# Seven more mixed pairs in the second half of two down projections, with row groups added into the residual stream by DMAs

## The chip, the cores and the metric

The program runs on one core of a Trainium2 chip. The metric is the device time of one execution in microseconds. The kernel before takes 2253.8 us (median of three runs, 2253.06 to 2253.91).

## What is computed

A decoder trunk over 256 tokens of width 2048 with two layers: an mLSTM layer and a differential-attention layer, each followed by a gated ConvFFN, with a residual stream `h` throughout and a final RMSNorm. The change touches only the ConvFFN's down projection (`@ w_down`, 5632 x 2048 in float32) and what is done with its result:

```python
def conv_ffn(xn, w_up, conv_w, conv_b, w_down):
    u = xn @ w_up
    ...                       # causal convolution of width 3 over the tokens
    gate, val = jnp.split(c, 2, axis=-1)
    return (jax.nn.silu(gate) * val) @ w_down

for layer in range(DEPTH):
    h = h + mixer_or_attention(h)
    h = h + conv_ffn(rms_norm(h, f_norm[layer]), w_up[layer], conv_w[layer], conv_b[layer], w_down[layer])
return rms_norm(h, final_norm)
```

## The kernel before

**Products in three passes.** Each float32 operand is split into a high part, rounded to the matmul's format, and the rest, so that a product is three matmuls: high by high, low by high, high by low. The activations are split once. The weights come in by `nc.sync` (queue SP) in blocks of 1 MB (`raw`, four buffers) and are split as they are needed: ACT copies the high part into a tile `w2` (five buffers), DVE subtracts it to get the low part (L376, L377 in `granule`).

**The down projection.** `conv_ffn` works in two halves of 22 k-tiles each (`part` 0 and 1). In each half the up projection makes `hidden[0..21]`, tiles of 128 channels by 256 tokens, and then `gemm_sevenths` makes the down product in groups `g` of 512 output columns, four groups a half. In the last layer's second half the fourth group is done otherwise (`finish`). A group's plain k-tiles go two at a time: twelve matmuls of 512 columns (L503) into two PSUM banks `a` and `b`, one for each half of the tokens.

**Seven products for eight.** A pair of k-tiles can be mixed instead: the pair, the two halves of the tokens and the two halves of the 512 columns make a 2 x 2 by 2 x 2 block product, which is done with seven block products where eight are usual. That is 21 matmuls of 256 columns (L493) in place of twelve of 512. Four sums of the hidden tiles are made ahead of it (`mix`), and four differences of the weights (`sevenths`: L449 to L451 on DVE into a buffer `diff` of the same four `raw` buffers). Seven weight blocks are then split instead of four: ACT L458 and DVE L459, three of them from `raw` and four from `diff`. `MIXED` names the k-tiles at which a mixed block of four k-tiles (two pairs) begins: 4, 12 and 20, the last with one pair only, so 10 of 22 k-tiles are mixed. Part of the mixed products goes into two more banks, `c` and `d` (`small_ps`, four such banks, which the transposes below use as well).

**Emptying a group.** `residual(norm)` returns the function that adds a finished group to `stream`, the residual in SBUF (128 tokens by 2 by 2048). `mixed_in` brings `c` and `d` in with one ACT copy (L572) and six DVE instructions (L573 to L579), and two more DVE adds (L587) bring in `a` and `b`. Then `norm.add(g)` begins the next layer's norm: two ACT squares of the new stream (L224), and in the next granule eight transposes on PE (L231), which ACT and DVE scale and split into `x_at` (L306, L307). In the last layer `evac_last` empties the groups; it makes the squares (L1074) and, two granules on, multiplies the stream by the final gain (L1075), with no transposes.

**The order.** `later(n, fn)` puts work off by `n` granules, counted by `tick()`. The Tile scheduler takes the program's order as priority and sets a fixed order for each engine; an engine runs its own queue in that order and waits on semaphores. Single matmuls, differences and adds of neighbouring blocks so come to stand between each other.

Of the kernel before, what the change touches and what calls it, by code (L numbers as in the profile page):

```python
# [37 lines left out]
NG = D // G  # L38
RAW = 4
OUT_AT = (8, 10)  # L40
MIXED = (4, 12, 20)
HL = 5
WARM, WARM_X = 28, 24
X_AT = (0, 2, 3, 5, 6, 8, 9)
# [24 lines left out]
def trunk(  # L69
# [394 lines left out]
    def gemm_sevenths(xs, mixed, w, col0, groups, evac, at):  # L464


        kn, raws = len(xs), {}
        for g in groups:
            a, b = (acc_ps.tile([P, 2 * T], F32, tag="acc", name="acc") for _ in range(2))
            c = d = None  # L470
            k0 = 0
            while k0 < kn:
                if k0 in at:
                    if c is None:
                        c, d = small_ps("mix"), small_ps("mix")
                    parts = sevenths(w, col0 + g * G, k0, min(2, (kn - k0) // 2))
                    for p, (b1, b2, b3, t1, t3, t2, t4) in enumerate(parts):
                        k = k0 + 2 * p
                        first, end = k == at[0], k0 == at[-1] and p == len(parts) - 1
                        (x0h, x0l, _), (x1h, x1l, _) = xs[k], xs[k + 1]  # L480
                        s1, s2, s3, s4 = mixed[k]
                        lo, hi = slice(0, P), slice(P, T)
                        c0, c1 = slice(0, T), slice(T, 2 * T)
                        ops = (((x0h[:, lo], x0l[:, lo]), b1, c[:, c0], first),
                               ((x1h[:, lo], x1l[:, lo]), b3, a[:, c1], False),
                               (s4, b2, a[:, c0], False),
                               (s1, t1, d[:, c0], first),
                               (s3, t3, d[:, c1], False),
                               (s2, t2, c[:, c1], False),
                               ((x1h[:, hi], x1l[:, hi]), t4, b[:, c1], False))  # L490
                        for (sh, sl), (th, tl), to, start in ops:
                            for o, (u, v) in enumerate(((sh, th), (sl, th), (sh, tl))):
                                pe.matmul(to, u, v, start=start and o == 0, stop=end and o == 2 and to is not a and to is not b, skip_group_check=True)  # L493
                        if p < len(parts) - 1:
                            tick()
                    k0 += 4
                else:
                    for i, (wh, wl) in enumerate(granule(w, col0 + g * G, G, k0, kn, raws, g)):
                        xh, xl, _ = xs[k0 + i]
                        for t, ps in enumerate((a, b)):  # L500
                            s = slice(t * P, (t + 1) * P)
                            for o, (u, v) in enumerate(((xh, wh), (xl, wh), (xh, wl))):
                                pe.matmul(ps, u[:, s], v, start=(k0 + i == 0 and o == 0), stop=(k0 + i == kn - 1 and o == 2), skip_group_check=True)  # L503
                    k0 += 2
                tick()
            evac(g, (a, b), (c, d))
# [71 lines left out]
        dve.tensor_tensor(both, both, u[1].rearrange("p (o n) -> p o n", o=1).broadcast_to([P, 2, T]), op=ALU.add)  # L578
        dve.tensor_tensor(stream[:, :, c0], d[:, :T].rearrange("p (o n) -> p o n", o=1).broadcast_to([P, 2, T]), stream[:, :, c0], op=ALU.add)  # L579

    def residual(norm):
        def evac(g, ps, mix=None):
            if mix is not None:
                mixed_in(g, mix)
            for t in range(2):
# [249 lines left out]
    def conv_ffn(layer, norm, evac_down, finish=None):  # L835
# [4 lines left out]
        for part in range(2):  # L840
# [20 lines left out]
            def evac_val(j, ps):  # L861
                pair = []
                for n in range(2):
# [5 lines left out]
                if 4 * (j // 2) in MIXED:  # L869
                    mixed[2 * j] = mix(pair)  # L870

            for j in range(half // 2):
# [1 line left out]
                gemm(norm.sets[0], w_up[layer], D_FF + part * half * P, [j], evac_val)  # L874
            rows = w_down[layer, part * half * P:(part + 1) * half * P]
            if part == 0:
                gemm_sevenths(hidden, mixed, rows, 0, range(NG), residual(None), MIXED)
            elif finish is None:
                gemm_sevenths(hidden, mixed, rows, 0, range(NG), evac_down, MIXED)
            else:  # L880
                gemm_sevenths(hidden, mixed, rows, 0, range(NG - 1), evac_down, MIXED)
                finish(hidden, rows)


# [156 lines left out]
    gemm_sevenths(outs, outs_mixed, m_w_out[0], 0, [NG - 1], residual(norm_f0), OUT_AT[:1])  # L1041

    norm_at = Norm([(gains, G_B), (gains, G_KV)], "at")
    conv_ffn(0, norm_f0, residual(norm_at))
    outs, outs_mixed = attention(norm_at)
    norm_f1 = Norm([(gains, G_F1)], "f1")
    gemm_tokens(outs, w_o[0], 0, range(2), residual(norm_f1), lead=2)
# [9 lines left out]
        return gain_rows[c0 // G][2][:, c0 % G:c0 % G + width]  # L1057

    def evac_last(g, ps, mix=None):
        if mix is not None:  # L1060
            mixed_in(g, mix)
# [6 lines left out]
        c0, width = g * G, G  # L1068
        if g == NG - 1:
            width = T  # L1070
        for t in range(2):
            rows = stream[:, t, c0:c0 + width]
            dve.tensor_tensor(rows, ps[t], rows, op=ALU.add)
            act.activation(tmp("sq").bitcast(BF16)[:, :width], rows, AF.Square, accum_out=norm_out.parts[:, t, g:g + 1])  # L1074
            later(2, lambda rows=rows: dve.tensor_tensor(rows, rows, gain_cols(c0, width), op=ALU.mult))  # L1075
        if g == NG - 1:
            later(1, sums_but_last)

    def sums_but_last():
        for t in range(2):  # L1080
# [60 lines left out]
```

## Time and profile before

| | |
|---|---|
| median of three runs | 2253.8 us |
| the profiled execution | 2253.21 us, span 2251.4 us, clock 0.999 |
| PE, DVE, ACT, POOL busy | 99%, 79%, 57%, 6% of the span |
| layer 0, second half: up projection | 761.45 to 1007.64 us |
| its down projection, groups 0 to 3 | 1007.64 to 1127.2 us |
| layer 1, second half: up projection | 1878.71 to 2124.20 us |
| its down projection, groups 0 to 2 | 2124.20 to 2212.41 us |

Times in the trace count from the first instruction. Busy PE counts matmuls, whose ends are modelled, since they are pipelined: how far apart they start says more than how long each is shown. A wait is put down to the engine, the line or the DMA whose semaphore came last.

### The profile page before, as it was taken

To read this page: it belongs to the slowest core of one execution; us is meant where nothing else is said; L and a number is where in the kernel's file an instruction comes from. 1 tells how busy PE (TensorE), PEld (TensorE's weight loads), DVE (VectorE), ACT (ScalarE), POOL (GpSimd) and SP (SyncE) were. 2 spreads that over 40 slices of the span, in tenths; PEclk is the share of its full clock that TensorE was granted. 3 is DMA by queue.
4 is the path that set the end of the run, shared out by engine and by line. 5 is a ranking of instruction groups with operands and counts; after the bars stand their busy time and mean duration, and the time that the engine had idled before them with its cause. 6 is when DMAs were issued, how large, how long until landed. Compare 5 with 4: busy or idle time off the path is not lost.

```text
span 2251.4 us, 33430 instructions
## 1 busy us (share of the span) xinstructions
PE 2239.6 (99%) x12843; PEld 1954.1 (87%) x12843; DVE 1789.7 (79%) x2964; ACT 1292.0 (57%) x1994; POOL 125.0 (6%) x305
## 2 busy tenths in 40 slices
PE   9999999999999999999999999999999999999998
PEld 9888888888888888888888888888888888888888
DVE  5756778887888877879998885677877988778896
ACT  5456655655555555656654556566555555556554
POOL 0014200000000000000022103200000000000000
PEclk9999999999999999999999999999999999999999
DMA  7554546555555755545566555465555457555464
GB/s 265 188 169 157 166 171 205 192 191 187 187 170 179 242 187 187 187 150 203 189 208 194 163 167 169 150 206 187 187 187 187 156 191 239 191 189 191 146 215 150
DMA packets 325348, 419.04 MB, mean 186 GB/s; under 512 B 9070, under 2 KB 238788, under 8 KB 325188
## 3 DMA queue, kind: packets, MB, share of 16 engines
q1 hardware_dynamic: 325156, 416.89, 56.4%
q8 instruction: 101, 1.65, 0.3%
q14 instruction: 59, 0.48, 0.1%
q10 hardware_dynamic: 32, 0.01, 0.0%
HBM read 414.77 MB, written 2.10 MB: 185 GB/s over the span
## 4 chain that ended last, share of the span: by engine, by line
PE 97%; DVE 1%; POOL 1%; issue 1%; ACT 0%; DMA 0%; DVEq 0%; SPq 0%; POOLq 0%
PE acc L411 54%; PE acc L503 16%; PE acc L437 12%; PE mix L493 6%; PE acc L493 4%; PE acc L634 2%; PE acc L521 1%; PE val_ps L335 1%; PE turn_ps L231 1%; PE as_ps L955 0%; DVE w L377 0%; POOL rs_u L279 0%; POOL rs_u L280 0%; DMA pos_i<-in_positions_dram 0%; POOL rs_u L281 0%
## 5 line engine op out<-in xcount | busy, mean ns | idle before, releaser
L377 DVE TENSOR_TENSOR w<-raw,w 128x1024 fp32r<-128x1024 f32 x679 | 825.9, 1220 | 280.1 <-ACT w L376 277.5
L376 ACT ACTIVATE w<-raw 128x1024 fp32r<-128x1024 f32 x679 | 713.9, 1058 | 491.7 <-PE acc L411 324.8
L411 PE MATMUL acc<-x_f,w 128*128 128x512 f32 (+1 forms) x5632 | 988.1, 337 | 0.0
L411 PEld LDWEIGHTS acc<-x_f,w 128*128 128x128 f32 x5632 | 861.7, 188 | 123.2
L503 PE MATMUL acc<-w,hid 128*128 128x512 f32 x1080 | 268.2, 394 | 0.0
L503 PEld LDWEIGHTS acc<-w,hid 128*128 128x128 f32 x1080 | 195.4, 188 | 39.0
L411 PE MATMUL acc<-x_at,w 128*128 128x512 f32 (+1 forms) x1024 | 182.1, 338 | 0.0
L411 PEld LDWEIGHTS acc<-x_at,w 128*128 128x128 f32 x1024 | 156.8, 188 | 22.2 <-issue 0.3
L458 ACT ACTIVATE w<-diff 128x1024 fp32r<-128x1024 f32 x89 | 94.1, 1057 | 111.1 <-DVE diff L451 81.7
L417 ACT ACTIVATE low<-acc 128x256 f32<-128x256 f32 x216 | 79.3, 386 | 135.4 <-PE acc L411 132.6
L459 DVE TENSOR_TENSOR w<-diff,w 128x1024 fp32r<-128x1024 f32 x89 | 108.7, 1221 | 40.9 <-ACT w L458 40.3
L437 PE MATMUL acc<-w,x_a 128*128 128x512 f32 x576 | 138.0, 396 | 0.0
L437 PEld LDWEIGHTS acc<-w,x_a 128*128 128x128 f32 x576 | 106.8, 188 | 24.2
L493 PE MATMUL mix<-w,mix 128*128 128x256 f32 x801 | 119.3, 281 | 0.0
L418 DVE TENSOR_TENSOR acc<-acc,low 128x256 f32<-128x256 f32 x216 | 84.5, 430 | 37.7 <-ACT low L417 37.3
L493 PEld LDWEIGHTS mix<-w,mix 128*128 128x128 f32 x801 | 107.0, 188 | 2.4 <-DVE w L459 0.2
L848 ACT ACTIVATE c<-u,conv 128x256 f32<-128x256 f32 x176 | 98.2, 593 | 5.5 <-DVE u L846 5.2
L939 POOL TENSOR_TENSOR sw<-sw,sin_t 32x256 f32<-32x256 f32 x32 | 42.0, 1328 | 1033.8 <-DVE sw L938 1022.5
L458 ACT ACTIVATE w<-raw 128x768 fp32r<-128x768 f32 x89 | 74.7, 840 | 37.9 <-PE acc L503 27.4
L437 PE MATMUL acc<-w,x_at 128*128 128x512 f32 x384 | 91.8, 396 | 0.0
L459 DVE TENSOR_TENSOR w<-raw,w 128x768 fp32r<-128x768 f32 x89 | 84.6, 951 | 2.8 <-ACT w L458 2.7
L493 PE MATMUL acc<-w,hid 128*128 128x256 f32 x450 | 86.3, 281 | 0.0
(302 smaller groups left out, 2320.4 us busy)
## 6 DMA issues: line engine op xcount, KB each, us to landing
raw<-in_w_up_dram SPq DMA_DIRECT2D x176, 1024.0 KB
raw<-in_w_down_dram SPq DMA_DIRECT2D x79, 1024.0 KB
raw<-in_m_w_in_dram SPq DMA_DIRECT2D x46, 1024.0 KB
raw<-in_w_kv_dram SPq DMA_DIRECT2D x32, 1024.0 KB
raw<-in_m_w_out_dram SPq DMA_DIRECT2D x16, 1024.0 KB
raw<-in_w_q_dram SPq DMA_DIRECT2D x16, 1024.0 KB
raw<-in_w_o_dram SPq DMA_DIRECT2D x16, 1024.0 KB
raw<-in_w_down_dram SPq DMA_DIRECT2D x15, 512.0 KB
```

Source lines behind the costliest of these rows:

```text
L376: act.activation(w2[:, :hc, 0], part, AF.Copy)
L377: dve.tensor_tensor(w2[:, :hc, 1], part, w2[:, :hc, 0].bitcast(F32), op=ALU.subtract)
L411: pe.matmul(to, a, b, start=(k == 0 and o == 0), stop=(k == kn - 1 and o == len(ops) - 1))
L417: act.activation(low, p[:, T:], AF.Copy)
L418: dve.tensor_tensor(p[:, :T], p[:, :T], low, op=ALU.add)
L437: pe.matmul(ps[t], a[:, s], b, start=(k == 0 and o == 0), stop=(k == kn - 1 and o == 2))
L458: act.activation(w2[:, :m, 0], src, AF.Copy)
L459: dve.tensor_tensor(w2[:, :m, 1], src, w2[:, :m, 0].bitcast(F32), op=ALU.subtract)
L493: pe.matmul(to, u, v, start=start and o == 0, stop=end and o == 2 and to is not a and to is not b, skip_group_check=True)
L503: pe.matmul(ps, u[:, s], v, start=(k0 + i == 0 and o == 0), stop=(k0 + i == kn - 1 and o == 2), skip_group_check=True)
L634: pe.matmul(ps[j], a, b, start=(k == 0 and o == 0 and j % 2 == 0), stop=(k == KD - 1 and o == 2), skip_group_check=True)
L848: act.activation(c, u, AF.Identity, bias=cw[:, 3, f:f + 1], scale=cw[:, 2, f:f + 1])
```

## The change

In the second halves the mixed blocks begin at k-tiles 2, 10 and 18, each with two pairs: 12 of 22 k-tiles instead of 10. The first halves stay as they are. A weight load covers the plain k-tiles between two mixed blocks, so a group has two plain ones in its first load (512 KB), then mixed blocks and plain blocks of four k-tiles in turn (1 MB each).

The first three groups of layer 0's second half and the first two of layer 1's are emptied by a new function, `landed`. ACT copies `a` and `b` into SBUF tiles, one ACT copy and four DVE adds make two more tiles from `c` and `d`, and four DMAs from POOL's queue add the four tiles into the stream. The norm's work on that group is put off by eight granules.

```diff
-MIXED = (4, 12, 20)
+MIXED = ((4, 12, 20), (2, 10, 18))
...
-                    for i, (wh, wl) in enumerate(granule(w, col0 + g * G, G, k0, kn, raws, g)):
+                    since = max([0] + [k + 4 for k in at if k < k0])
+                    until = min([kn] + [k for k in at if k > k0])
+                    for i, (wh, wl) in enumerate(granule(w[since * P:until * P], col0 + g * G, G, k0 - since, until - since, raws, g)):
...
+    def landed(g, ps, mix, then):
+        (a, b), (c, d) = ps, mix
+        u = tmp("mx")
+        a2, b2, x, y = (block(F32, f"land_{n}") for n in "abxy")
+        act.activation(x[1], c[:, :T], AF.Copy)
+        dve.tensor_tensor(u, c[:, T:], x[1], op=ALU.add)
+        act.activation(a2[2], a, AF.Copy)
+        dve.tensor_tensor(y[1], d[:, T:], u, op=ALU.add)
+        act.activation(b2[2], b, AF.Copy)
+        dve.tensor_tensor(x[0], d[:, :T], u, op=ALU.add)
+        dve.tensor_tensor(y[0], d[:, :T], y[1], op=ALU.add)
+        for t, rows in ((0, a2), (1, b2), (0, x), (1, y)):
+            pool.dma_start(stream[:, t, g * G:(g + 1) * G], rows[2], accum_op=ALU.add)
+        later(8, then)
...
-    def residual(norm):
+    def residual(norm, by_dma=0):
         def evac(g, ps, mix=None):
+            if g < by_dma:
+                landed(g, ps, mix, lambda: norm.add(g))
+                return
...
-    conv_ffn(0, norm_f0, residual(norm_at))
+    conv_ffn(0, norm_f0, residual(norm_at, 3))
...
     def evac_last(g, ps, mix=None):
...
+        if g < 2:
+            landed(g, ps, mix, lambda: summed(g, G))
+            return
```

Up to the second half of layer 0 every engine's order stays as it was. Three places show how the order changes.

DVE at the boundary between groups 0 and 1 of layer 0. `w_10062` and `w_10065` before, `w_10044` and `w_10047` after, are the first splits of group 1's first mixed block, from `raw` and from `diff`. Before:

```order
L459 TENSOR_TENSOR w_10062<-raw,w_10062 128x3x256
L451 TENSOR_TENSOR diff<-raw,diff 128x2x256
L573 TENSOR_TENSOR mixed<-mix,mixed 128x256
L575 TENSOR_TENSOR stream<-mix,stream 128x256
L574 TENSOR_TENSOR mixed<-mix,mixed 128x256
L576 TENSOR_TENSOR stream<-stream,mixed 128x256
L578 TENSOR_TENSOR stream<-stream,mixed 128x512
L459 TENSOR_TENSOR w_10065<-diff,w_10065 128x4x256
```

The same place after; L589 to L594 are `landed`:

```order
L459 TENSOR_TENSOR w_10044<-raw,w_10044 128x3x256
L450 TENSOR_TENSOR diff<-raw,diff 128x2x256
L589 TENSOR_TENSOR mx<-mix,land_x 128x256
L451 TENSOR_TENSOR diff<-raw,diff 128x2x256
L591 TENSOR_TENSOR land_y<-mix,mx 128x256
L593 TENSOR_TENSOR land_x<-mix,mx 128x256
L594 TENSOR_TENSOR land_y<-mix,land_y 128x256
L459 TENSOR_TENSOR w_10047<-diff,w_10047 128x4x256
```

The four adds of `landed` stand where five of the emptying's adds stood, and the adds of `a`, `b` and the rest, which followed later, are gone.

PE some 8 us into group 1 of layer 0, where the transposes of group 0's new stream (L231) stand. `w_10118` before and `w_10100` after are the split plain k-tiles behind the first mixed block. Before:

```order
L493 MATMUL acc<-w_10068,mix 128x256 x3
L503 MATMUL acc<-w_10118,hid_8427 128x512 x2
L493 MATMUL acc<-w_10071,hid_8218 128x256
L503 MATMUL acc<-w_10118,hid_8427 128x512 x2
L231 MATMUL turn_ps<-ident,stream 128x128 x2
L493 MATMUL mix<-w_10062,hid_7989 128x256 x3
L493 MATMUL mix<-w_10065,mix 128x256 x9
```

After (L505 is the line L503 of before):

```order
L505 MATMUL acc<-w_10100,hid_8217 128x512 x2
L493 MATMUL mix<-w_10053,mix 128x256 x5
L493 MATMUL acc<-w_10053,hid_8008 128x256
L505 MATMUL acc<-w_10100,hid_8217 128x512 x2
L231 MATMUL turn_ps<-ident,stream 128x128 x2
L493 MATMUL mix<-w_10136,hid_8637 128x256 x2
L231 MATMUL turn_ps<-ident,stream 128x128 x6
L505 MATMUL acc<-w_10100,hid_8217 128x512 x2
```

The transposes stand at about the same distance from the boundary as before, ahead of the matmuls with the low part of `w_10100`, and what they read now comes from the adding DMAs.

POOL, which has nothing in this stage before, now has the following rows (with the semaphores that each waits for; `DMASW0` and `DMASW1` are those of the first two DMAs; the last row belongs to group 1):

```order
L596 DMA stream<-land_a 128x512 [waits DVE_49,PE_49,Activation_49]
L596 DMA stream<-land_b 128x512 [waits DVE_49,PE_49,Activation_49]
L596 DMA stream<-land_x 128x512 [waits DMASW0_49,DVE_49]
L596 DMA stream<-land_y 128x512 [waits DMASW1_49,DVE_49]
L596 DMA stream<-land_a 128x512 [waits PE_49,Activation_49]
```

The third DMA waits for the landing of the first, the fourth for that of the second, since they add into the same rows.

More of the change, by code (lines that the diff above doesn't have):

```diff
@@ L868, in evac_val @@
                     pair.append(c)
-                if 4 * (j // 2) in MIXED:
+                if any(k <= 2 * j < k + 4 for k in MIXED[part]):
                     mixed[2 * j] = mix(pair)
@@ L876, in conv_ffn @@
             if part == 0:
-                gemm_sevenths(hidden, mixed, rows, 0, range(NG), residual(None), MIXED)
+                gemm_sevenths(hidden, mixed, rows, 0, range(NG), residual(None), MIXED[part])
             elif finish is None:
-                gemm_sevenths(hidden, mixed, rows, 0, range(NG), evac_down, MIXED)
+                gemm_sevenths(hidden, mixed, rows, 0, range(NG), evac_down, MIXED[part])
             else:
-                gemm_sevenths(hidden, mixed, rows, 0, range(NG - 1), evac_down, MIXED)
+                gemm_sevenths(hidden, mixed, rows, 0, range(NG - 1), evac_down, MIXED[part])
                 finish(hidden, rows)
@@ L1059, in evac_last @@
     def evac_last(g, ps, mix=None):
-        if mix is not None:
-            mixed_in(g, mix)
         if g == 0:
```

16 lines of the change are left out of this document (10 added, 6 removed).

## The prediction

> **What bounds the kernel now.** I read the page's busy shares and the shares of the chain that ended last, then the chain in order of time around the second half of layer 0's ConvFFN, then busy time by stage, the costs of the instructions that the change adds and removes, and last the traffic of the DMA engines and of POOL.
>
> The page (busy us, share of the span, count; below it the shares of the chain):
>
> ```profile
> span 2251.4 us, 33430 instructions
> PE 2239.6 (99%) x12843; PEld 1954.1 (87%) x12843; DVE 1789.7 (79%) x2964; ACT 1292.0 (57%) x1994; POOL 125.0 (6%) x305
> PE 97%; DVE 1%; POOL 1%; issue 1%; ACT 0%; DMA 0%; DVEq 0%; SPq 0%; POOLq 0%
> ```
>
> The end is set by TensorE. Time is saved only by taking matmul time away, and lost wherever PE is made to wait. The chain in order of time (start, length, what) shows what a matmul costs in the stage that is changed:
>
> ```profile
> 1007.64 5.59 PE acc L503 x24
> 1013.23 0.35 PE mix L493 x3
> ...
> 1018.19 0.94 PE acc L503 x4
> ...
> 1036.86 5.59 PE acc L503 x24
> ...
> 1045.52 0.22 PE turn_ps L231 x2
> ...
> 1067.00 5.58 PE acc L503 x24
> ```
>
> 24 plain matmuls take 5.59 us, so 0.2329 us each. The 42 matmuls of one mixed block of four k-tiles stand between 1013.23 and 1018.19: 4.96 us, 0.1181 each. The pieces join without a gap. A group is 72 plain and 105 mixed matmuls, 16.77 + 12.40 = 29.17 us; measured 29.22 from 1007.64 to 1036.86. The next group takes 30.14, since eight transposes (0.11 us each) stand in it.
>
> By stage (length; busy time and count of PE, PEld, DVE, ACT, POOL; clock; DMA share; GB/s), the up projection of layer 0's second half and its groups 0 to 2, then groups 0 and 1 of layer 1:
>
> ```profile
> 761.45:1007.64 246.19, 246.19 (x1408) 215.06 (x1407) 196.14 (x329) 144.92 (x222) 0.00 (x0) 1.00 0.59 193
> 1007.64:1036.86 29.22, 29.22 (x179) 25.95 (x178) 27.36 (x41) 17.36 (x23) 0.00 (x0) 1.00 0.53 178
> 1036.86:1067.00 30.14, 30.14 (x187) 26.85 (x186) 28.40 (x38) 19.60 (x28) 0.00 (x0) 1.00 0.53 178
> 1067.00:1097.12 30.12, 30.12 (x186) 26.84 (x186) 28.18 (x37) 19.41 (x28) 0.00 (x0) 1.00 0.58 192
> 2124.20:2153.31 29.11, 29.11 (x179) 25.91 (x178) 27.38 (x41) 17.37 (x23) 0.00 (x0) 1.00 0.53 176
> 2153.31:2182.50 29.19, 29.19 (x176) 25.82 (x175) 26.60 (x34) 17.56 (x23) 0.00 (x0) 1.00 0.63 211
> ```
>
> PE is full, and in the groups DVE is at 91 to 94%: a second engine stands close behind the first. POOL is idle here.
>
> **The change part by part.** *The matmuls.* In seven groups (four of layer 0, three of layer 1) one more pair of k-tiles is mixed: 12 plain matmuls go (2.795 us), 21 mixed ones come (2.480). That is 0.315 us a group, 2.2 us in all, straight from the path.
>
> *VectorE's work for it.* Groups of instructions (busy us, mean ns of one; the last row is from the instructions in order of time):
>
> ```profile
> L377 DVE TENSOR_TENSOR w<-raw,w 128x1024 fp32r<-128x1024 f32 x678 | 825.2, 1221 | 280.1 <-ACT w L376 277.5
> L459 DVE TENSOR_TENSOR w<-diff,w 128x1024 fp32r<-128x1024 f32 x89 | 108.7, 1221 | 40.9 <-ACT w L458 40.3
> L459 DVE TENSOR_TENSOR w<-raw,w 128x768 fp32r<-128x768 f32 x89 | 84.6, 951 | 2.8 <-ACT w L458 2.7
> L449 DVE TENSOR_TENSOR diff<-raw 128x1024 f32<-128x1024 f32 x37 | 45.1, 1219 | 4.2 <-DMA raw<-in_w_down_dram 3.3 <-DMA raw<-in_w_o_dram 0.8
> L451 DVE TENSOR_TENSOR diff<-raw,diff 128x512 f32<-128x512 f32 x37 | 25.3, 684 | 0.2
> L587 DVE TENSOR_TENSOR stream<-acc,stream 128x512 f32<-128x512 f32 x40 | 25.7, 682 | 0.1
> L573 DVE TENSOR_TENSOR mixed<-mix,mixed 128x256 f32<-128x256 f32 x20 | 8.3, 417 | 0.9 <-ACT mixed L572 0.8
> L572 ACT ACTIVATE mixed<-mix 128x256 f32<-128x256 f32 x20 | 7.6, 382 | 17.2 <-PE mix L493 17.2
> L224 ACT ACTIVATE sq<-stream 128x512 bf16<-128x512 f32 x32 | 19.7, 618 | 3.9 <-DVE stream L587 3.8
> 1015.43 2.35 DVE L377 TENSOR_TENSOR w<-raw,w 128x1024 fp32r<-128x1024 f32 x2
> ```
>
> The last row (two splits in 2.35 us) says that neighbours overlap by 0.09 us, so each counts as its mean less 0.09. A pair that becomes mixed drops one L377 (1.13) and adds two L459 (0.86 + 1.13) and a full set of differences in place of a half one (about +1.05): +1.9 us a group. Emptying a group costs now four DVE adds of 256 columns and four of 512 (L578, L579 and L587 twice, taken as 0.59 each): 1.31 + 2.36 = 3.7 us. An emptied-by-DMA group costs four of 256: 1.3. So where the adding DMAs come in, DVE gets 2.4 back for 1.9: 28.40 becomes about 27.9 in 29.8 us, still 94%. Group 0 has no emptying inside its window: 27.36 + 1.9 = 29.3 in 28.85. The cover there is the lead: the first mixed split of that group runs long before PE uses it at 1013.23:
>
> ```profile
> 1003.16 0.95 DVE L459 TENSOR_TENSOR w<-raw,w 128x768 fp32r<-128x768 f32 x1
> PEld mix L493 <- DVE w L459: 0.2, 1, 0.2
> ```
>
> A lead of 9 us pays an excess of 0.4, so group 0 costs nothing. The second row (layer 1's second half, the one wait of PE on a split) says that the lead does run out within a group: without the lead this term is on the path. ACT gets two copies of 512 columns for a group (2 x 0.62) and has 10 us idle in it: hidden. One more `mix` in each second half (about 2 us of DVE) lies in the up projection, where DVE is at 80%.
>
> *Just after a group boundary* DVE stands still until the last mixed matmul is done, since its landing adds now stand ahead of the first split by differences. From that matmul: ACT's `land_x` to 0.43, DVE's four adds and L451 to 2.4, ACT's difference split (behind `land_a` and `land_b`) to 2.7, then DVE: two L459 of differences, one of raw, one L449, and the split for k-tile 6 at 2.7 + 1.13 + 0.86 + 1.13 + 1.13 + 1.13 = 8.1. PE, by the new order, needs that split after 8 + 4 plain and 42 mixed matmuls: 7.75 us in layer 1, and 0.2 to 0.9 later in layer 0, where transposes stand ahead of it. Bounds: nothing (if the split comes 0.4 sooner than this count) to 1 us a group (if the adds wait for `land_x` as long again). I take 0.4 in two groups of layer 1: +0.8 us.
>
> *The adding DMAs.* For each half of the tokens two DMAs add into the same rows, the second (`land_x`, `land_y`) issued only after the first has landed. In layer 0 the transposes of the new stream stand in PE's fixed order 8 + 4 plain and 40 mixed matmuls after the last mixed one: 1.86 + 0.93 + 4.72 = 7.5 us (groups 1; 8.0 and 7.75 for the next two), and the other half's 0.5 us later. Behind them queue all of PE's matmuls. With d for one adding DMA, `land_a` issues at 0.43 + 0.62 = 1.05 us, and the first pair has landed at 1.05 + 2d. No row shows an adding DMA. The nearest are loads: when a 1 MB load is issued and first used, and the traffic beside it (40 slices of 0.25 us from 1036):
>
> ```profile
> 1058.03 0.37 SPq L446 DMA_DIRECT2D raw<-in_w_down_dram  x1
> 1063.07 1.23 DVE L449 TENSOR_TENSOR diff<-raw 128x1024 f32<-128x1024 f32 x1 [0.76 <-DMA raw<-in_w_down_dram]
> GB/s 295 426 401 426 393 401 410 401 393 115 0 0 0 0 0 0 0 0 0 0 0 0 66 0 0 0 0 0 0 0 0 0 90 74 131 131 279 401 410 401
> ```
>
> 5.04 us for 1.05 MB, of which 2.56 at 410 GB/s: 2.5 us are fixed. A plain 256 KB would take 2.5 + 0.64 = 3.1. Adding reads the target as well, at most once more the bytes: 3.7. Lower bound: the bytes alone, 0.64; upper: the whole load's 5.04. I take 3.4, between the two prices scaled from the load. In the third row the DMA engines are empty for 5 us after the boundary, so the first DMAs meet no load; a load comes 7 us in, and may meet the second. Then the first half lands at 7.85: PE waits 0.35, 0 and 0.1 us; the other half (0.6 later, plus POOL's issue 0.2) lands near 8.6: 0.25, 0 (its transposes stand 6 us later there) and 0.3. Sum 1.0 us in layer 0. In layer 1 no transpose waits; only ACT's squares and DVE's gain products do, and the splits behind them are needed some 15 us in: nothing up to a landing at about 12.
>
> *Sum.* -2.2 + 0.8 + 1.0 = -0.4 us. The profiled execution took 2253.21 (span 2251.4 and 1.8 around it), 0.6 under the median of 2253.8; so 2252.8 against itself, 2253.4 against the median.
>
> **The rivals.** A run can tell 0.2%, 4.5 us, from no change.
>
> A: the saving comes whole. If an adding DMA is no dearer than the plain price of 3.1, the pair lands at 7.25, ahead of every transpose; with the scheduler's fillers covering the split, 2251.6. For it: the empty DMA engines. Against: the second half still lands near 8.0, with no margin. The Trainium skill (DMA: Bandwidth & Descriptors, Anatomy of one DMA — SWDGE (gpsimd) path) gives 2.0 us plus bytes over 436 GB/s for such a DMA, an estimate of 2.6 here; by that the first wait is gone and the sum would be -1.4. No run so far shows it.
>
> B, slower: the adding DMAs are slow on POOL's side. Each microsecond of d puts two on PE's wait in three groups. The three first-half waits add up to 6d - 20.1; with 1.3 for the rest (0.8 of splits, 0.5 of second halves), less 2.2 saved, 4.5 us are lost from d = 4.3 on. At d = 5 it is 2253.8 + 9.9 + 1.3 - 2.2 = 2262.8. What speaks for it is POOL beside a busy DVE (ns: min/median/max):
>
> ```profile
> L281 POOL TENSOR_SCALAR rs_u<-rs_u x48: 192/193/2092, 145.8 to 1444.0; 128x2 f32<-128x2 f32 x48
> 210.56 2.09 POOL L281 TENSOR_SCALAR rs_u<-rs_u 128x2 f32<-128x2 f32 x1
> 211.06 1.20 DVE L377 TENSOR_TENSOR w<-raw,w 128x1024 fp32r<-128x1024 f32 x1
> L757 POOL MEMSET mv<- x16: 95/101/221, 47.4 to 215.6; 128x2 f32 x16
> ```
>
> A two-column POOL instruction that takes 0.19 us took 2.09 while DVE worked; one that only writes never took over 0.22. If making the descriptors is held up like the first, d gains 1 to 2 us. The Trainium skill (SBUF — State Buffer, Who interferes with whom) says that a VectorE instruction with two SBUF inputs holds up a GpSimd one that reads SBUF, not one that only writes, and infers that descriptors need only the write side. The trace agrees on reading and writing; on descriptors no run here shows anything, so B keeps a quarter.
>
> C: the mixed pair costs PE more than its share, or something else waits for the landing, and the result is within 2 us above no change.
>
> **How the numbers follow.** Forecast (small waits, 2252.3 to 2256): 0.42. A: 0.25. B: 0.26, most of it between 2258.3 and 2263. C: 0.04. Over 4.5 us faster needs twice the whole saving: 0.03. So faster 0.03, same 0.71 (forecast, A, C), slower 0.26. The range reaches from A, 2251.4, to d of almost 5, 2262; some 0.17 is left out.
>
> **What would show it.** Group 0 of either layer near 28.9 us. In layer 0's later groups, transposes (L231) that wait for a DMA into the stream, under 1 us each: if over 2, B. If PE waits on L377 some 8 us after a boundary in layer 1, the split's term is right; if nowhere, A. The prediction is wrong if an adding DMA takes outside 3.1 to 4.3 us from issue to use, or if ACT, held at the squares, starves PE through later splits.

## The result and the profile after

The changed kernel takes 2291.2 us (median of 4 runs, 2289.6 to 2294.0), the kernel before, on the same chip, 2253.7 (2253.1 to 2253.9): a ratio of 1.0168 with a 95% interval of 1.0155 to 1.0180. It is 37.5 us slower; the forecast was 2253.4, with 2262.0 as the upper end.

The page of the changed kernel:

```profile
span 2287.9 us, 33625 instructions
PE 2253.6 (99%) x12906; PEld 1966.0 (86%) x12906; DVE 1796.8 (79%) x2961; ACT 1301.7 (57%) x2013; POOL 142.4 (6%) x325
PE 77%; issue 17%; DMA 2%; DVE 2%; ACT 1%; POOL 1%; DVEq 0%; SPq 0%; ACTq 0%; POOLq 0%
```

PE still reads 99%, though the span grew by 36.5 us: matmuls at a lower clock count as busy too. What gives it away is the chain: adding DMAs, DVE and ACT are now pieces of it. Most of PE's fall from 97% to 77% is no loss, though. Followed back to the first adding DMA, the chain goes on along POOL's queue, which had stood idle, and counts this one piece as "issue" (start, length, what), 15.6% of the span in which PE was busy:

```profile
681.64 357.27 issue
```

To place the loss I cut both executions into four stretches at matmuls that both kernels have: the second half's down projection of layer 0 (from the up projection's last matmul to the third of the attention's first product), the start of the attention (the next 226 matmuls of that product), everything from there to layer 1's last up projection, and the end. Columns as in the stages of the prediction; before, then after:

```profile
1007.37:1127.43 120.06, 120.06 (x737) 106.90 (x735) 111.25 (x150) 77.33 (x106) 0.00 (x0) 1.00 0.57 189
1127.43:1168.51 41.08, 41.08 (x241) 35.91 (x239) 36.20 (x76) 23.30 (x37) 7.54 (x4) 1.00 0.68 216
1168.51:2123.92 955.41, 955.41 (x5369) 830.19 (x5368) 761.92 (x1306) 545.86 (x868) 66.62 (x132) 1.00 0.56 183
2123.92:2251.42 127.50, 119.13 (x797) 109.09 (x795) 102.85 (x149) 66.26 (x93) 0.00 (x0) 0.98 0.52 174
```

```profile
1007.40:1148.48 141.08, 128.06 (x772) 113.56 (x771) 112.20 (x142) 82.56 (x114) 10.57 (x12) 0.94 0.63 187
1148.48:1193.43 44.95, 41.23 (x240) 35.80 (x239) 36.80 (x76) 23.62 (x38) 7.66 (x4) 1.00 0.64 198
1193.43:2150.72 957.29, 957.29 (x5369) 830.85 (x5368) 764.74 (x1312) 546.22 (x869) 66.56 (x132) 1.00 0.56 182
2150.72:2287.90 137.18, 123.07 (x824) 113.10 (x822) 103.75 (x144) 70.36 (x100) 6.94 (x8) 0.96 0.59 181
```

So +21.0, +3.9, +1.9 and +9.7 us. In layer 0's down projection PE idles 13.0 us (length less busy), and its clock is 0.94 over 141 us, which is another 8.5 us of matmul time. The adding DMAs tell why. The chain around the end of layer 0's group 0 (start, length, what):

```profile
1038.95 0.74 POOL stream L596
1039.68 5.42 DMA stream<-land_b
...
1045.63 5.77 DMA stream<-land_y
...
1051.44 1.54 PE turn_ps L231 x6
1052.98 5.88 PE acc L505 x20
```

The group's first copy (ACT, L588) starts at 1037.7. The second pair's last DMA has landed 13.7 us later; near 8.6 was predicted. Six transposes that take 0.66 us before take 1.54, and twenty plain matmuls 5.88, though at 0.2329 each they need 4.66. The waits between 1030 and 1150 us (engine, line, what it waited for: us, times, longest), and then those of layer 1's end:

```profile
ACT sq L224 <- DMA stream<-land_x: 11.4, 3, 5.3
ACT sq L224 <- DMA stream<-land_y: 9.6, 3, 6.4
...
PE turn_ps L231 <- DMA stream<-land_x: 7.8, 3, 4.2
...
PE turn_ps L231 <- DMA stream<-land_y: 4.1, 3, 1.6
```

```profile
ACT sq L1105 <- DMA stream<-land_x: 9.3, 2, 6.9
...
PE mix L493 <- ACT w L458: 5.3, 2, 3.9
ACT sq L1105 <- DMA stream<-land_y: 5.2, 2, 3.7
```

In layer 0 transposes wait for the landing. In layer 1 there are none; there ACT waits, at the squares, and the splits queued behind them (L458) reach PE late. The clock in three pieces behind such waits, and between the second and the third the piece behind a wait of 3.1 us at the attention's start (PE is busy; the number after POOL's is the clock):

```profile
1051.44:1055.60 4.16, 4.16 (x13) 3.58 (x14) 1.96 (x4) 3.19 (x6) 0.00 (x0) 0.51 0.50 193
1091.70:1096.40 4.70, 3.88 (x21) 3.64 (x20) 3.65 (x4) 4.70 (x7) 0.00 (x0) 0.65 0.02 9
...
1159.67:1164.00 4.33, 4.33 (x27) 3.81 (x28) 2.91 (x16) 1.23 (x4) 0.00 (x0) 1.00 0.79 246
...
2230.70:2236.40 5.70, 5.68 (x26) 5.68 (x27) 5.70 (x6) 4.28 (x5) 0.00 (x0) 0.50 0.21 42
```

In three places (the first and the last piece, and one at 1124.6 us) waits that add up to 3.9 to 5.4 us are followed by 4 to 6 us at half the clock, which costs another 2 to 3. The Trainium skill (TensorE: Matmul & The Clock Gate, What's actually happening) states a clock of one half after an idle window of about 3.4 us, until a busy one has passed. The traces agree on the half, but give no such length: the piece at 0.65 follows waits of 1.2 and 0.8 us, and behind 3.1 us at the attention's start the clock stayed at 1.00. What decides it these runs don't show.

### The profile page after: what moved, and what is told of

Its sections match the earlier page's. It is cut to its first block, busy times and chain, and to the rows that moved or that the text cites. A ratio compares the mean times of both kernels' runs of the same rounds, so it can differ in the third digit from the quotient of the medians.

```text
span 2287.9 us, 33625 instructions
## 1 busy us (share of the span) xinstructions
PE 2253.6 (99%) x12906; PEld 1966.0 (86%) x12906; DVE 1796.8 (79%) x2961; ACT 1301.7 (57%) x2013; POOL 142.4 (6%) x325
## 4 chain that ended last, share of the span: by engine, by line
PE 77%; issue 17%; DMA 2%; DVE 2%; ACT 1%; POOL 1%; DVEq 0%; SPq 0%; ACTq 0%; POOLq 0%
PE acc L411 42%; PE acc L437 12%; PE acc L505 11%; PE mix L493 4%; PE acc L493 3%; PE acc L656 2%; DMA stream<-land_y 1%; DMA stream<-land_b 1%; PE acc L523 1%; PE turn_ps L231 1%; PE val_ps L335 1%; DVE w L377 1%; DVE w L459 0%; POOL rs_u L279 0%; DVE diff L449 0%
## 5 line engine op out<-in xcount | busy, mean ns | idle before, releaser
L377 DVE TENSOR_TENSOR w<-raw,w 128x1024 fp32r<-128x1024 f32 x672 | 817.4, 1221 | 275.0 <-ACT w L376 272.4
L376 ACT ACTIVATE w<-raw 128x1024 fp32r<-128x1024 f32 x672 | 706.3, 1058 | 475.8 <-PE acc L411 327.8
L505 PE MATMUL acc<-w,hid 128*128 128x512 f32 x996 | 253.2, 400 | 0.0
L505 PEld LDWEIGHTS acc<-w,hid 128*128 128x128 f32 x996 | 182.5, 191 | 36.1
L458 ACT ACTIVATE w<-diff 128x1024 fp32r<-128x1024 f32 x96 | 101.4, 1056 | 106.3 <-DVE diff L451 74.4
L459 DVE TENSOR_TENSOR w<-diff,w 128x1024 fp32r<-128x1024 f32 x96 | 117.4, 1223 | 51.9 <-ACT w L458 51.5
L493 PE MATMUL mix<-w,mix 128*128 128x256 f32 x864 | 135.9, 286 | 6.6 <-ACT w L458 6.4
L493 PEld LDWEIGHTS mix<-w,mix 128*128 128x128 f32 x864 | 119.5, 192 | 12.0 <-ACT w L458 8.0
L458 ACT ACTIVATE w<-raw 128x768 fp32r<-128x768 f32 x96 | 80.4, 838 | 33.4 <-PE acc L505 19.4
L493 PE MATMUL acc<-w,hid 128*128 128x256 f32 x492 | 99.4, 285 | 0.0
L459 DVE TENSOR_TENSOR w<-raw,w 128x768 fp32r<-128x768 f32 x96 | 91.5, 953 | 3.7 <-ACT w L458 3.0
```

The source lines that it names most:

```text
L376: act.activation(w2[:, :hc, 0], part, AF.Copy)
L377: dve.tensor_tensor(w2[:, :hc, 1], part, w2[:, :hc, 0].bitcast(F32), op=ALU.subtract)
L458: act.activation(w2[:, :m, 0], src, AF.Copy)
L459: dve.tensor_tensor(w2[:, :m, 1], src, w2[:, :m, 0].bitcast(F32), op=ALU.subtract)
```

## The experiments

Two theories at first: the late landing is the whole loss, or the third block's splits are. The stretches of each run against the kernel before (change in us, from the same four cuts through the profiled execution, which lies up to 5 us from the median; "start" is the loss ahead of the first stretch, where it is over 1):

| run | median us | ratio, 95% | layer 0 down | attention's start | middle | layer 1 down |
|---|---|---|---|---|---|---|
| changed kernel | 2291.2 | 1.0155 to 1.0180 | +21.0 | +3.9 | +1.9 | +9.7 |
| e1_mix: third block alone | 2273.4 | 1.0070 to 1.0100 | +7.1 | +3.9 | +0.5 | +6.0 |
| e2_dma: DMAs alone | 2270.4 | 1.0057 to 1.0087 | +8.8 | +4.2 | -0.1 | +0.7 |
| e4_hold | 2272.8 | 1.0067 to 1.0101 | +5.3 | +8.3 | +1.5 | +4.6 |
| e5_hold_pe | 2280.2 | 1.0104 to 1.0134 | +8.7 | +8.6 | +1.5 | +9.5 |
| e14_later | 2270.1 | 1.0053 to 1.0087 | +7.7 | +8.9 | -0.2 | +2.7 |
| e6_plain | 2272.7 | 1.0065 to 1.0105 | +7.3 | +5.3 | +1.9 | +6.3 |
| e13_other | 2271.4 | 1.0064 to 1.0094 | +5.5 | +5.5 | +1.8 | +6.5 |
| e15_other10 | 2259.8 | 1.0015 to 1.0037 | -0.2 | +4.9 | +1.7 | -0.1 |
| e17_thin | 2257.3 | 1.0011 to 1.0033 | +0.6 | +1.3 | +0.8 | -0.7 |
| e8_pos | 2266.2 | 1.0042 to 1.0076 | +6.4 | +0.2 | -0.1 | +6.3 |
| e11_pos_hold | 2278.6 | 1.0093 to 1.0123 | +10.8 | +7.7 | -1.3 | +3.0 |
| e19_space | 2261.0 | 1.0020 to 1.0044 | +1.1 | +6.8 | -1.3 | +1.6 |
| e16_att | 2257.1 | 1.0006 to 1.0025 | -0.2 | +2.0 | +1.7 | -0.1 |
| e18_pool | 2291.1 | 1.0148 to 1.0176 | +18.5 (start +8.3) | 0.0 | +6.4 | +5.0 |
| e20_real | 2258.6 | 1.0013 to 1.0033 | +2.2 | +2.0 | +0.2 | +1.0 |

**Each half of the change alone.**

```diff
 e1_mix
-    conv_ffn(0, norm_f0, residual(norm_at, 3))
+    conv_ffn(0, norm_f0, residual(norm_at))
-        if g < 2:
+        if g < 0:
             landed(...)
 e2_dma
-MIXED = ((4, 12, 20), (2, 10, 18))
+MIXED = ((4, 12, 20), (4, 12, 20))
```

> 12 of 22 k-tiles mixed in the seven groups, but every group emptied as before, with no adding DMA. Theory (the loss of 37.5 us comes from the late landing of the adding DMAs): no transposes wait for a DMA; the 2.2 us of matmul time are saved, and VectorE, which now has 1.9 us more in each group and no relief, reaches 28.4 + 1.9 = 30.3 us in a group of 29.8, so it gives back 0.5 us in six groups or less: 2251 to 2256. Rival 1 (the loss comes from the splits and differences of the third mixed block, which come too late for TensorE): 2280 to 2292.

> The adding DMAs stay, the second halves mix 10 of 22 k-tiles as before. Theory: the landing has its whole price without the third block, and no matmul is saved: 2285 to 2297. Rival 1 (late splits of the third block): 2252 to 2260.

Both theories fell: either half alone costs 17 to 20 us. Mixing alone puts PE on splits in layer 0, each wait short:

```profile
PE acc L493 <- DVE w L459: 1.6, 3, 0.5
PE acc L493 <- ACT w L458: 1.2, 4, 0.5
```

**The landing without its waits.** The readers of a landed group are kept behind in the order (e4_hold, on all engines; e5_hold_pe, on PE alone; e14_later, by 13 granules), or read other columns of the stream (e13_other, and e15_other10 with the old blocks).

```diff
 e4_hold (as_written ties each instruction behind the one written ahead of it on its engine)
+            with as_written():
                 self.squares(g)
 ...
 e14_later
-        later(8, then)
+        later(9 if g == 2 else 13, then)
 e13_other, e15_other10
-                act.activation(..., stream[:, t, g * G:(g + 1) * G], AF.Square, ...)
+                act.activation(..., stream[:, t, r * G:(r + 1) * G], AF.Square, ...)   # r = 3
-                    pe.transpose(..., stream[:, t, (i + c) * P:...], ident)
+                    pe.transpose(..., stream[:, t, (r + c) * P:...], ident)            # r = 12 + i % 4
 (in layer 1 the squares and gain products read group 2's columns)
```

> The changed kernel, but the squares, transposes and gain products that need a landed group are kept where they are written, nine granules (some 22 us) behind the group's end, on each of the three engines, and not moved forward. Theory: every adding DMA has landed 13.7 to 16.4 us after the group's end, so nothing waits, TensorE's clock stays up, and what is left is the saving and the 0.8 us of late splits: 2251 to 2254. Rival 2 (the adding DMAs cost by being there: they take the DMA engines from the weight loads or hold up VectorE, whoever waits for them): above 2265.

> As the kernel with everything held behind, but TensorE's transposes alone are held; ScalarE's squares may move forward as in the changed kernel. Theory: the 13 us of waiting transposes go, but ScalarE stands at a square until the DMA has landed and the splits behind it come late for TensorE: layer 1 keeps its 7.9 us, and layer 0 keeps 1.5 to 7 us in each of three groups: 2262 to 2280. If ScalarE's wait is covered in layer 0: 2259 to 2262. If the squares cost nothing anywhere: 2251 to 2254.

> The changed kernel, with the true readers of a landed group held behind by 13 granules (9 for group 2 of layer 0) instead of 8, on all engines, so that ScalarE, which runs some 10 us ahead of TensorE, does not reach a square before the landing either. Held by 8 it took 2272.8. Theory: no wait for a landing anywhere; what stays is the start of the attention (up to 8 us in the held kernels) and what the third block costs in late splits: 2255 to 2266. Rival (the DMAs disturb by being there): 2270 to 2276.

> The changed kernel with the same DMAs and the same third block, but nobody waits for a landing: the transposes and squares that should read a landed group read another group's columns of the stream (the output is not the reference's). Splits up what is left when the landing is free. If VectorE's relief by the DMAs pays for the third block, as the prediction had it: no late splits, 2251 to 2256 (up to 3.7 us of it at the start of the attention, where group 3 is still emptied by VectorE late). If the third block costs late splits even so: 2260 to 2268. Rival (the DMAs disturb by being there): 2270 or more.

> The same, and the second halves mix 10 of 22 as before: the adding DMAs alone, with nobody waiting for them and VectorE relieved of 2.4 us a group. If the DMAs cost only through those who wait: 2252 to 2258 (0 to 4 us at the start of the attention). Rival (they disturb): 2262 to 2270, as the run with DMAs and 10 of 22 whose readers wait (2270.4).

Holding back on all engines saves 18 us, where the theory asked for all 37. (In e4_hold ACT still waits 11.5 us at layer 0's squares; in e14_later no engine but POOL waits for a landing.) With PE alone held, layer 1 keeps its +9.5: there it is ACT that waits. By their times e4_hold, e13_other and e14_later fall into the range of the rival by which the DMAs disturb, and e15_other10 lies between its two ranges, so the stretches have to decide. With all twenty DMAs, old blocks and no reader (e15_other10), the two down projections take what they took before:

```profile
1007.77:1127.63 119.86, 119.86 (x736) 106.62 (x735) 103.62 (x135) 77.31 (x108) 10.57 (x12) 1.00 0.70 211
1127.63:1173.62 45.99, 42.93 (x240) 37.11 (x239) 37.51 (x79) 24.97 (x41) 7.64 (x4) 0.96 0.65 206
2130.73:2258.12 127.39, 118.99 (x797) 109.14 (x795) 98.02 (x141) 68.43 (x97) 6.88 (x8) 0.99 0.60 190
```

With the old blocks, then, the DMAs cost nothing there by being there, only through those who wait; the attention's start (+4.9) comes below. With the third block added to that (e13_other) 5.7 and 6.6 us are lost again, with PE busy 121.0 and VectorE 110 of 125.6 us in layer 0's. Late splits, in layer 0 (lines of e13_other, two above those of the changed kernel):

```profile
PE mix L495 <- ACT w L460: 2.5, 4, 0.9
PE acc L507 <- DVE w L379: 2.0, 2, 1.0
```

The second row is the DMAs' doing in part. VectorE stands at a difference until its weight load has come, and the split behind it is late (chain, VectorE, PE):

```profile
1048.19 9.26 DMA raw<-in_w_down_dram
1057.54 1.23 DVE L451 TENSOR_TENSOR diff<-raw 128x1024 f32<-128x1024 f32 x1 [1.91 <-DMA raw<-in_w_down_dram]
1059.95 4.92 PE L507 MATMUL acc<-w,hid 128*128 128x512 f32 x20 [1.00 <-DVE w L379]
```

Beside adding DMAs such loads took 8.8 to 9.3 us, where the prediction's took 5.04, and three waits of PE of 1.0 us (two in layer 0, one in layer 1) stand behind them. They are not the whole: e1_mix, with no adding DMA, loses 7.1 us in layer 0 without a wait of VectorE for a load there.

**What the landing is made of.** e6_plain drops `accum_op=ALU.add`, nothing else.

> The changed kernel whose four DMAs a group write into the stream without adding (so the second overwrites the first and the stream is not the reference's): same queue, same order, same waits. Theory (adding makes each DMA occupy the DMA engines longer, 256 KB at 160 to 200 GB/s where a load runs at 410): landing from issue 2.5 to 4 us instead of 3.3 to 9.3, the last of a group 9 to 11 us after the group's end instead of 13.6 to 16.4, time 2274 to 2285. Rival (POOL's queue and the loads beside it set the landing, not the adding): landing as in the changed kernel, time 2287 to 2294.

The bus in both kernels, in 40 slices over the 6 us around the first issues, at whose start a weight load ends (share of the DMA engines in tenths, GB/s), the adding DMAs first, then the plain ones:

```profile
DMA  9999995310000000499999999949999999982011
GB/s 410 423 410 410 410 369 219 137 41 14 0 0 0 0 0 0 82 177 191 177 177 205 205 191 191 177 55 259 191 177 191 205 191 164 191 150 28 0 14 14
```

```profile
DMA  9998300000049979179898104000000000599962
GB/s 437 423 382 341 123 0 0 0 0 0 0 191 410 410 300 410 28 300 382 355 410 300 28 27 109 0 0 0 0 0 0 0 0 0 246 437 437 382 246 82
```

Both fill the DMA engines; two adding DMAs together mostly move 150 to 205 GB/s, plain copies up to 410. From issue to landing (us, min/median/max), all adding DMAs of the changed kernel, then `land_a` and `land_y` of the plain ones:

```profile
DMA to landing us min/median/max: 3.3/5.6/9.3
```

```profile
DMA to landing us min/median/max: 3.1/3.4/6.0
DMA to landing us min/median/max: 3.6/4.7/7.7
```

The theory was half right: plain DMAs land sooner, and the time falls by 18 us, further than expected (2274 was the lower end); yet plain ones that meet weight loads still take 6.0 to 7.7 us. Adding and meeting loads both make the landing long; the second is read from the groups that had loads beside them, and no run moves the loads. In e6_plain PE still waits 4.5 us for landings in layer 0 and 2.8 behind ACT's squares in layer 1, yet its stretches are about those of e13_other, in which nobody waits: waits for a landing and late splits partly stand in for each other.

**Work or place.** e17_thin leaves two of three subtractions of a block out (and splits the first difference twice in their place); e8_pos, e11_pos_hold and e19_space move the blocks; e18_pool gives those two subtractions to POOL. e17_thin and e18_pool do so in every mixed block of the kernel, not in the seven groups alone.

```diff
 e17_thin (on e13_other)
-        dve.tensor_tensor(d[:, :, 2], b[:, :, 2], d[:, :, 0], op=ALU.subtract)
-        dve.tensor_tensor(d[:, :, 3], b[:, :, 3], d[:, :, 2], op=ALU.subtract)
 e8_pos (on e1_mix), e11_pos_hold (on e4_hold)
-MIXED = ((4, 12, 20), (2, 10, 18))
+MIXED = ((4, 12, 20), (4, 10, 16))
 e19_space (on e13_other): (4, 12, 18)
 e18_pool (on e1_mix)
-        dve.tensor_tensor(d[:, :, 2], b[:, :, 2], ...)    # and d[:, :, 3]
+        pool.tensor_tensor(d[:, :, 2], b[:, :, 2], ...)
```

> No adding DMA, 12 of 22 k-tiles mixed, but the blocks of the second halves begin at k-tiles (4, 10, 16) instead of (2, 10, 18): four plain k-tiles stand between the group's end and the first mixed block, as before the change, and the last block is followed by two plain ones. Mixing at (2, 10, 18) without the DMAs took 2273.4 us; beyond its matmuls TensorE lost 8.5 us in layer 0's second half and 7.2 in layer 1's to late splits. Theory (it is the place: the first block comes before VectorE has emptied the group and made the differences): most of these 15.7 us go, 2252 to 2260. Rival (VectorE simply has too much to do, some 30.3 us in a group of 29.8, wherever the blocks stand): 2265 to 2276.

> The changed kernel with its DMAs, the readers of a landed group held behind as in the run that held all three engines (2272.8 us), and the blocks at (4, 10, 16). If place and landing are two causes that add up, this removes the 5.2 us (layer 1) and 6.7 us (layer 0) of late splits that were left there, and perhaps the longer wait of 8.3 us at the start of the attention: 2253 to 2262. If VectorE's load is the cause, the DMAs relieve it and it should still be no worse than 2266. Rival (the adding DMAs disturb whatever stands beside them): 2268 to 2275.

> The kernel with the DMAs, 12 of 22 k-tiles and nobody waiting for a landing (2271.4 us), without the second and third subtraction of every mixed block (L450 and L451, 0.68 us each for two pairs; the splits take the first difference twice, each half by itself; the output is not the reference's). In it TensorE lost 6.9 us in layer 0's second half and 7.5 in layer 1's to late splits, though VectorE was busy only 88% there. Theory (a mixed block asks VectorE for 6.9 us of work for 4.96 us of matmuls, and three blocks with one or two plain granules between them leave no time to catch up): with 5.5 to 5.7 us a block these waits go, 2251 to 2258 with what the attention's start costs. Rival (ScalarE or TensorE itself sets the pace of the third block): 2264 to 2272.

> As the kernel with the DMAs, 12 of 22 k-tiles and nobody waiting for a landing (2271.4 us, blocks at (2, 10, 18)), with the blocks at (4, 12, 18): two plain granules before the first block and between the first two, one before the last. If only the place at the group's end makes splits late: most of the 14.4 us go, 2255 to 2262. If three blocks in a group are too dense for VectorE wherever they stand: 2266 to 2274.

> 12 of 22 k-tiles mixed in the seven groups and no adding DMA, as in the run of 2273.4 us, but POOL, which is idle there, makes the second and third subtraction of every mixed block (L450 and L451), so that a block asks VectorE for 5.5 us instead of 6.9. The output is the reference's. Theory (VectorE's work for a mixed block is what comes late): a good part of the 15.7 us of late splits goes, 2252 to 2264; at the lower end this is the version that could match the kernel before. Rival: POOL's two subtractions in series (a 32x256 one took 1.3 us there) or its port beside VectorE make the differences later still: 2266 or more.

Less work per block removes the late splits: layer 1 takes 0.7 us less than before, of 0.95 saved in matmuls, and layer 0 0.6 more. (The ten runs of e17_thin spread from 2252.8 to 2266.1; the profiled one took 2254.6. Without the two subtractions the way from a load to its last split is shorter too; which of the two counts was not separated.) So does another place, nearly: at (4, 12, 18) the two stretches are 1.1 and 1.6 us longer than before instead of 5.5 and 6.5. What PE still waited for in layer 0 of e19_space:

```profile
PE mix L495 <- ACT w L460: 0.4, 1, 0.4
PE acc L507 <- DVE w L379: 0.2, 1, 0.2
```

My rival "too dense wherever they stand" is refuted for the relieved VectorE. (4, 10, 16) was no better than (2, 10, 18) in the two down projections, in e8_pos (+12.7 us there against 13.1 in e1_mix; its time, 7 us shorter, comes from other stretches and lies in its rival's range) or with the DMAs in e11_pos_hold, where my sum of two causes missed by 16 us. It has one plain granule between all three blocks; (2, 10, 18) has one over the group's end, where the emptying falls, and (4, 12, 18) one inside the group. POOL is no way out. The two subtractions of 128 by 512 take 2.1 and 2.0 us there, and VectorE's splits beside it get longer (L459 from `raw` 951 ns before, 1150 now):

```profile
L450 POOL TENSOR_TENSOR diff<-raw,diff 128x512 f32<-128x512 f32 x44 | 94.0, 2135 | 1400.9 <-ACT hid L300 510.5 <-DVE sum L533 478.1 <-DVE diff L449 167.8
```

**The start of the attention.** Here either half of the change alone loses 3.9 or 4.2 us. In the changed kernel VectorE empties group 3 (L575 to L609) with more splits for the attention between the adds:

```profile
1153.24 0.69 DVE L580 TENSOR_TENSOR stream<-stream,mixed 128x512 f32<-128x512 f32 x1
1154.91 1.23 DVE L377 TENSOR_TENSOR w<-raw,w 128x1024 fp32r<-128x1024 f32 x1 [0.98 <-ACT w L376]
1156.05 0.68 DVE L581 TENSOR_TENSOR stream<-mix,stream 128x512 f32<-128x512 f32 x1
1157.70 1.23 DVE L377 TENSOR_TENSOR w<-raw,w 128x1024 fp32r<-128x1024 f32 x1 [0.97 <-ACT w L376]
1158.84 1.28 DVE L609 TENSOR_TENSOR stream<-acc,stream 128x512 f32<-128x512 f32 x2
```

Those splits wait for ACT, ACT for a `w2` buffer that PE has yet to free, and the transposes wait 3.1 us for L609. e16_att keeps the later splits behind the adds.

```diff
 e16_att (on e15_other10)
+        with tc.issue_after(emptied[0].ins) if emptied[0] and len(emptied) > 6 else nullcontext():
             dve.tensor_tensor(w2[:, :hc, 1], part, w2[:, :hc, 0].bitcast(F32), op=ALU.subtract)
```

> The run with the adding DMAs alone that nobody waits for (10 of 22 k-tiles, 2259.8 us), with one order changed: from the sixth split of the attention's first product on, VectorE may make splits only after the two adds that empty group 3 into the stream. There they lost 3.1 us to transposes that waited for those adds, with up to four splits between them, and 4.9 us in that stretch in all. If the order is the cause, the rest is before's: 2252.5 to 2255. If the stretch is slow for another reason (ScalarE's squares, a clock that falls): 2257 to 2261.

It gave back 2.9 of 4.9 us; at 2257.1 it is at the lower edge of the second expectation. The wait of the transposes fell from 2.4 us (not 3.1, as I had expected from e15_other10) to 1.2, and the clock, 0.60 for 4.2 us behind the longer wait, stayed up. The order is the larger part; the rest is again a copy on ACT that stands behind four splits. In both runs the chain there comes through a load of `w_q` that took 10.6 and 10.9 us, so slow loads may have a share in it; no run tells.

**All of it, with the reference's output.** e20_real: blocks at (4, 12, 18), two landed groups a layer held by 13 granules, and the order of e16_att.

> What the runs taught, with the reference's output: blocks of the second halves at (4, 12, 18), groups 0 and 1 of either layer emptied by adding DMAs and their readers held behind by 13 granules, and at the start of the attention group 3's two adds ahead of all but the first splits. By the stretches of the runs that had one of these each: layer 0's second half 1 to 4 us longer than before (its group 2 is emptied by VectorE again), the attention's start 2 to 6 longer, layer 1's 1.6 longer: 2257 to 2265. If the causes hide each other and fall away together: 2252 to 2255. Not expected: under 2252.

2258.6 us, as the sum of the stretches had it: 33 of the 37.5 us are back, and the kernel before is still faster, 1.0013 to 1.0033. No version here beats it.

## Why the prediction was wrong, step by step

By the stretches the loss splits up so: DMAs that nobody waits for, -0.3 us in the down projections (e15_other10); the third block on top of them, 5.7 + 6.6 (e13_other less e15_other10); the landing's waits, 15.5 + 3.2 (changed kernel less e13_other); the attention's start 3.9; the middle 1.9. That is 36.5 us, the growth of the span. The terms are differences between runs and depend on the order in which the parts come: with the old blocks the landing's waits cost 9.0 and 0.8 us (e2_dma less e15_other10) instead of 15.5 and 3.2, and without the DMAs the third block costs 13.1 (e1_mix) instead of 12.3. In the changed kernel itself PE waits for splits only 1.1 us in layer 0, against 4.5 in e13_other: while it waits for a landing, VectorE catches up.

- **The matmuls: right.** 2.2 us were to be saved, 0.95 of it in layer 1; in e17_thin PE is busy 0.96 less there (118.17 against 119.13 us), and the stretch is 0.65 shorter, with 0.23 of waits left. Group 0 was right too: it costs what its matmuls do, since the 63 plain and 128 mixed ones that start in this row (some are its neighbours') make 29.8 of its 30.0 us:

```profile
1007.52:1037.53 30.01, 30.01 (x194) 27.13 (x193) 27.40 (x40) 17.20 (x22) 0.00 (x0) 1.00 0.53 172
```

- **VectorE's splits: failed.** I took 0.8 us, 1 us a group at most. Measured where nobody waits for a landing: 12.3 net, 14.5 with the saving, 2.1 a group, some of it through slow loads. The wait that the 0.8 us stood for does exist (in layer 1 of e1_mix PE waits on L377 twice, 0.48 us, some 9 us after a boundary), but it is the small part. The failed step set VectorE's work against PE's over a whole group (27.9 in 29.8 us). A mixed block asks it for 6.9 us by the means of its seven instructions (6.3 with 0.09 off for each neighbour) in 4.96 of PE, and it can be ahead by five `w2` tiles only, of which a block takes four. So what stands between two blocks counts, whatever the group's sum says: the same three blocks cost 5.5 and 6.5 us at (2, 10, 18) and 1.1 and 1.6 at (4, 12, 18) (e13_other, e19_space), and with 1.2 to 1.4 us less work a block 0.6 and -0.7 (e17_thin). How much must stand there is not shown, since (4, 12, 18) too has two blocks one granule apart; that the buffers set the lead is argued, not tried.
- **The adding DMAs: the first right, the pairs failed.** d = 3.4 was the time of a group's first (3.3 to 3.7 us in the three groups where hardly a load was near, 5.8 and 6.0 in the other two); none ran all by itself. The failed step is "the first pair has landed at 1.05 + 2d, the other half 0.6 later": it gave each DMA the engines for itself. Two run at a time and fill them, and the second pair meets the loads. The last landed 13.7 to 16.4 us after the group's first copy, not 8.6. The trace of before had both facts: a load fills the bus, and the next one comes 7 us after a boundary.
- **Layer 1's "nothing up to a landing at about 12": the landing came at 13.7 and 16.4**, so the condition was not met, and whether 12 is the limit was not tried. ACT at its squares starved PE, as the last sentence of the prediction named it; it had no price there.
- **Left out: the clock.** Of the landing's 15.5 us in layer 0, 8.4 are PE's idle time (13.0 less the 4.6 of e13_other); the rest is PE's busy time, longer by 7.1 at a clock of 0.94 instead of 1.00. The prediction counted a wait as its own length.
- **Left out: group 3.** I looked at the order at the boundaries that the change names, not at the next one, where the order moved as well: 3.9 us.

Rival B had the sign and the criterion (transposes waiting over 2 us), but not the cause. POOL's part is short and steady, though VectorE is busy beside it (`land_b`, which follows at once, takes 1.18 to 1.21 us):

```profile
L596 POOL DMA_DIRECT2D stream<-land_a x5: 850/859/1054, 1038.9 to 2213.7; - x5
L596 POOL DMA_DIRECT2D stream<-land_y x5: 854/859/859, 1045.6 to 2221.4; - x5
```

That agrees with the inference of the Trainium skill (SBUF — State Buffer, Who interferes with whom) that making descriptors is not held up by VectorE's reads. Rival A's estimate of 2.6 us by the Trainium skill (DMA: Bandwidth & Descriptors, Anatomy of one DMA — SWDGE (gpsimd) path) lies among the best plain ones (2.3 to 3.6 us, the least of each tile in e6_plain), not the adding ones.

The middle's +1.9 us stays open: PE is busy throughout in both, and the runs fall between -1.3 and +1.9 there, apart from e18_pool, with no pattern that I could name.

## What to carry to other kernels

Count a DMA's landing with everything that shares its engines in that window, and ask who stands in order behind the reader: a wait on ACT is paid by PE, and a wait of PE can be paid again in clock. Where an engine is within a tenth of full, compare its work with the bound engine's block by block, not by the sum over a stage, and take prices apart with care: two causes of waiting can hide each other or make each other dearer. A saving of 2 us that needs work on four engines to move has more ways to lose than to win: look at every boundary where the order changes, the next stage's first one too.

## What the hardware showed that I had not expected

- Two adding DMAs of 256 KB from SBUF to SBUF together move about 180 GB/s with the DMA engines full; the same copies without adding move up to 410. A weight load beside adding DMAs took up to 9.3 us.
- Behind waits of PE of 3.9 to 5.4 us in all, matmuls of 512 columns came every 0.43 us instead of 0.23, for 4 to 6 us; behind one of 3.1 us the clock stayed up.
- POOL subtracting beside VectorE costs both: 2.1 us for 128x512, where VectorE takes 0.68, and VectorE's splits go from 951 to 1150 ns.
